# mLSTM gates turned by TensorE, and all retention state steps on GpSimd, in a two-block layer stack

## The chip, the cores and the metric

The program runs on one core of a Trainium2 chip. A core has TensorE (PE, matrix products and transposes into PSUM), VectorE (DVE), ScalarE (ACT), GpSimd (POOL) and SyncE (SP, which here issues the DMAs); each has its own list of instructions and runs it in order, and semaphores tie the lists together. The metric is the time of one execution in microseconds on the device (us).

## The reference, cut to what matters

Two blocks of two layers each work on 512 tokens of width 1024 in float32. The change touches the mLSTM's gates in the first block and the retention's states in the second.

```python
# first block, token_mixer: 4 mLSTM heads beside sliding-window attention
gates = mif + gate_bias                      # [512, 8]
log_i, log_f = gates[..., :4], log_sigmoid(gates[..., 4:])
ht = mlstm_chunkwise(mq_h, mk_h, mv_h, log_i, log_f)
# in it, for each chunk of 128 tokens:
bc = cumsum(log_f)                           # along the tokens
m_row = max(b + m, max(dlog))                # running maximum along the tokens
w_inter = exp(b + m - m_row); ws = exp(b_last - b + li - m_new)

# second block, bidirectional_retention: 6 heads, 4 chunks of 128 tokens, forward and backward
s_new = s * c_dec + einsum('bhcd,bhce->bhde', kb * k_dec, vb)
y = einsum(a, vb) + einsum('bhid,bhde->bhie', qb, s) * q_dec
```

## The kernel before

**Products.** Each float32 matrix product is made of three matmuls on split operands (L447 to L449: high by high, low by high, high by low). A weight tile comes by DMA on SP (L371), ACT rounds it to its high part (L385), DVE takes the low part (L386). PE's results lie in PSUM, in four buffers "mm" for products and four "ax" for transposes, scores and the like. Small work tiles named u come from a ring of 31 buffers (`NU`, L27): a new tile gets the buffer that has been free longest, and its first writer waits until the last user of that buffer is done.

**What sets the order.** The program is written out by a host loop. The products are emitted in units; each unit and each transpose moves a clock `s.now` forward by an estimate, and `s.later(delay, fn)` puts side work on a heap which is emitted once that clock has gone `delay` ns further. So a delay decides between which units, and behind which other instructions of its engine, a piece of side work stands. On the chip each engine then runs its list in that order, whatever the true times are.

**Gates, first block** (`gates1` to `gates4`, once a layer). `gates1` makes log_i and log_f as columns (tokens on partitions). To get rows (heads on partitions, tokens along the row), `gates2` writes them to device memory in eight DMAs whose elements are 4 bytes (L912), `gates3` reads them back as two tiles of 4x512 (L920). `gates4` then runs a scan over the tokens (the cumulative sum, L935), a subtraction (L936) and a small copy (L937); 1800 ns later `stab` has the second scan (the running maximum, L940) and four sums and differences (L941 to L944); `fin` writes five row tiles to device memory (L950), `cols` reads two of them back as columns in eight DMAs (L957), and `ends` takes their exponential (L962). `mlstm` fetches the other rows spread over partitions, and starts when the last product of its values is there.

**Beside it** in the same stretch run the units of the attention (scores by L581, the maximum by DVE's L1049, the exponential by ACT's L1054, the normalisation by L1059, L1060 and L593, transposes by L577, their copies by ACT's L1075 and DVE's L1077, the product with the values by L589) and `ev_qk`, which reads a product out of its "mm" buffer four times: ACT's L1243 and three convolution taps on DVE (L1246, 511, 510 and 509 columns).

**Retention, second block** (`x_layer`, once a layer). Tiles `st[0]` to `st[3]` hold the state at each chunk, the forward half on partitions 0 to 63 (`f`), the backward half on 64 to 127 (`b`). A step (`step`, L1357 and L1358) multiplies one half by its decay and adds it to the next tile: three steps forward on DVE, three backward on POOL, written out alternately. `ret_chunk` follows: two products of the queries with their decays (L1477), transposes of keys and queries whose copies are L1488, transposes of the decayed queries (L577, `dturn`), score products (L581), masks (L1511) and the output (L581).

**Modulation** (`mod`). When a layer's modulation is ready, `keep` writes four rows to device memory by four DMAs on SP in a row (L867).

Of the kernel before, what the change touches and what calls it, by code (L numbers as in the profile page):

```python
# [17 lines left out]
P = 128  # L18
# [188 lines left out]
class Net:  # L207
# [591 lines left out]
    def mod(s):  # L799
# [53 lines left out]
        def ready(l):  # L853
# [8 lines left out]
            def keep():  # L862
                gd = s.dram([2, 2, D], "mgate")
                for w in range(2):
                    for i in range(2):
                        o = (3 * i + 2) * 8
                        nc.sync.dma_start(gd[w, i].rearrange("(j p) -> p j", p=P), md[:, w, o:o + 8])  # L867
                s.mgate[l] = gd
# [22 lines left out]
    def gates1(s, l, zg, got):  # L891
# [13 lines left out]
        gd = s.dram([8, 512], "grow")  # L905
        s.later(6000, lambda: s.gates2(g3, lf3, gd, got))

    def gates2(s, g3, lf3, gd, got):
        nc = s.nc
        for i, src in enumerate((g3, lf3)):  # L910
            for t in range(NT):
                nc.sync.dma_start(gd[i * 4:i * 4 + 4, t * P:(t + 1) * P].rearrange("h p -> p h"), src[:, t, :4])  # L912
        s.later(3000, lambda: s.gates3(gd, got))

    def gates3(s, gd, got):
        nc = s.nc
        rows = []
        for i in range(2):
            r = s.u((4, 512))
            nc.sync.dma_start(r, gd[i * 4:i * 4 + 4])  # L920
            rows.append(r)
        s.later(2800, lambda: s.gates4(rows, got))

    def gates4(s, rows, got):
        nc = s.nc
# [13 lines left out]
        def stab():  # L939
# [5 lines left out]
            s.later(2600, fin)  # L945

        def fin():
            gr = s.dram([5, 4, 512], "gfin")
            for i, x in enumerate((bm, a, m, wi, ws)):
                nc.sync.dma_start(gr[i], x)  # L950
            s.later(2600, lambda: cols(gr))

        def cols(gr):
            co = s.ti(32)
            for i in range(2):
                for c in range(NT):
                    nc.sync.dma_start(co[:, i * 16 + c * 4:i * 16 + c * 4 + 4],  # L957
                                      gr[i, :, c * P:(c + 1) * P].rearrange("h p -> p h"))
            s.later(2800, lambda: ends(gr, co))

        def ends(gr, co):
            nc.scalar.activation(co[:, :16], co[:, :16], AF.Exp, scale=-1.0)  # L962
# [130 lines left out]
    def mlstm(s, gates, qk, vm, gs, outs):  # L1093
# [7 lines left out]
        def bring(hp):  # L1101
            for src, dst in ((4, wsb), (3, wib)):
# [5 lines left out]
        def bring_m(hp):  # L1108
            for i in range(2):
                w = s.u()  # L1110
                nc.sync.dma_start(w, gr[2, hp * 2 + i].partition_broadcast(P))
# [686 lines left out]
    def x_layer(s, l, xs, norm, res, mid, groups_of, sinks_of, parts):  # L1798
# [62 lines left out]
        yield from s.until(lambda: len(kv) == NT)  # L1861
# [259 lines left out]
```

## Time and profile before

| | |
|---|---|
| median of 3 runs | 2812.58 us (2811.86 to 2814.61) |
| profiled execution | 2813.32 us, span 2811.5 us |
| busy: PE | 2705.4 us, 96% of the span |
| busy: DVE | 1895.9 us, 67% |
| busy: ACT | 1167.0 us, 42% |
| busy: POOL | 572.0 us, 20% |
| mean granted clock of TensorE | 0.989 of full speed |

How to read it: the span is the time from the first to the last instruction of the profiled execution. PE is busy nearly all of it; its idle time is what waits cost. The list of waits says for an engine and line on whom they ended; the timeline has every instruction with its start, its length and the idle time before it, and the name behind the arrow is the instruction at which the awaited semaphore was last seen to rise, which can be the neighbour of the one that mattered.

### The profile page before, as it was taken

To read this page: it belongs to the slowest core of one execution; us is meant where nothing else is said; L and a number is where in the kernel's file an instruction comes from. 1 tells how busy PE (TensorE), PEld (TensorE's weight loads), DVE (VectorE), ACT (ScalarE), POOL (GpSimd) and SP (SyncE) were. 2 spreads that over 40 slices of the span, in tenths; PEclk is the share of its full clock that TensorE was granted. 3 is DMA by queue.
4 is the path that set the end of the run, shared out by engine and by line. 5 is a ranking of instruction groups with operands and counts; after the bars stand their busy time and mean duration, and the time that the engine had idled before them with its cause. 6 is when DMAs were issued, how large, how long until landed. Compare 5 with 4: busy or idle time off the path is not lost. (4 is left out here: it accounts for less than half of the span.)

```text
span 2811.5 us, 38854 instructions
## 1 busy us (share of the span) xinstructions
PE 2705.4 (96%) x14526; PEld 2291.8 (82%) x14526; DVE 1895.9 (67%) x3414; ACT 1167.0 (42%) x2098; POOL 572.0 (20%) x616
## 2 busy tenths in 40 slices
PE   8899999998999999999999999999999999999998
PEld 6678888876788887788788888888888888888887
DVE  6767777777668678857657787778646556664544
ACT  4555332445554323555443633223336442442433
POOL 2222000042230000234153220221102335201011
PEclk9999999999999999999999999999999999999999
DMA  5633444425334464333332243333513322333332
GB/s 166 89 90 124 148 153 140 145 77 86 91 112 153 149 124 158 123 118 113 105 92 82 87 139 117 105 117 109 87 49 98 116 73 73 97 118 100 98 98 68
DMA packets 135804, 308.22 MB, mean 110 GB/s; under 512 B 38024, under 2 KB 44040, under 8 KB 135616
## 3 DMA queue, kind: packets, MB, share of 16 engines
q1 hardware_dynamic: 135040, 304.69, 37.3%
q8 instruction: 115, 1.88, 0.3%
q10 hardware_dynamic: 576, 1.05, 0.1%
q14 instruction: 73, 0.60, 0.1%
HBM read 303.44 MB, written 2.24 MB: 109 GB/s over the span
## 5 line engine op out<-in xcount | busy, mean ns | idle before, releaser
L385 ACT CAST wh<-wr 128x1024 fp32r<-128x1024 f32 (+2 forms) x455 | 461.3, 1015 | 578.4 <-PE mm L449 259.6
L447 PE MATMUL mm<-nh,wh 128*128 128x512 f32 (+1 forms) x1776 | 671.6, 378 | 3.6 <-DVE nh L187 3.6
L448 PE MATMUL mm<-nl,wh 128*128 128x512 f32 (+1 forms) x1776 | 666.9, 375 | 0.9 <-POOL nl L188 0.4
L449 PE MATMUL mm<-nh,wl 128*128 128x512 f32 (+1 forms) x1776 | 665.9, 375 | 0.0
L386 DVE TENSOR_TENSOR wl<-wr,wh 128x1024 fp32r<-128x1024 f32 (+2 forms) x455 | 572.3, 1263 | 112.5 <-ACT wh L385 112.1
L617 DVE SCALAR_TENSOR_TENSOR u<-mm,vec,u 128x511 f32<-128x511 f32 (+2 forms) x440 | 305.9, 695 | 234.6 <-ACT u L612 163.5
L447 PE MATMUL mm<-wh,u 128*128 128x512 f32 (+1 forms) x1176 | 460.5, 392 | 2.1 <-ACT u L632 1.9
L448 PE MATMUL mm<-wl,u 128*128 128x512 f32 (+1 forms) x1176 | 454.7, 387 | 2.6 <-DVE wl L386 2.4
L449 PE MATMUL mm<-wh,u 128*128 128x512 f32 (+1 forms) x1176 | 454.4, 386 | 2.2 <-DVE u L633 1.5
L447 PEld LDWEIGHTS mm<-nh,wh 128*128 128x128 f32 x1776 | 336.6, 190 | 66.3 <-issue 4.8
L449 PEld LDWEIGHTS mm<-nh,wl 128*128 128x128 f32 x1776 | 336.0, 189 | 60.4
L448 PEld LDWEIGHTS mm<-nl,wh 128*128 128x128 f32 x1776 | 336.6, 190 | 58.1 <-DVE nl L188 1.0
L447 PEld LDWEIGHTS mm<-wh,u 128*128 128x128 f32 x1176 | 221.9, 189 | 46.8 <-ACT u L632 2.7
L449 PEld LDWEIGHTS mm<-wh,u 128*128 128x128 f32 x1176 | 221.6, 188 | 46.0 <-DVE u L633 3.5
L448 PEld LDWEIGHTS mm<-wl,u 128*128 128x128 f32 x1176 | 222.0, 189 | 45.3 <-DVE wl L386 5.0
L447 PE MATMUL mm<-wh,nh 128*128 128x384 f32 (+2 forms) x512 | 191.1, 373 | 17.2 <-DVE t L934 10.8
L577 PE MATMUL ax<-ident,u 128*128 128x128 f32 x930 | 137.4, 283 | 50.6 <-DVE u L154 18.3
L449 PE MATMUL mm<-wh,nl 128*128 128x384 f32 (+2 forms) x512 | 182.0, 355 | 1.5 <-POOL nl L188 1.5
L448 PE MATMUL mm<-wl,nh 128*128 128x384 f32 (+2 forms) x512 | 181.7, 355 | 0.0
L577 PEld LDWEIGHTS ax<-ident,u 128*128 128x128 f32 x930 | 108.5, 144 | 80.9 <-issue 25.0
L737 POOL TENSOR_TENSOR x<-x,u 128x512 f32<-128x512 f32 x64 | 103.2, 1613 | 342.6 <-DVE u L736 341.4
L572 POOL TENSOR_TENSOR t<-t,mhalf 128x1 f32<-128x1 f32 (+2 forms) x76 | 63.3, 835 | 508.1 <-DVE t L570 507.8
(248 smaller groups left out, 3703.9 us busy)
## 6 DMA issues: line engine op xcount, KB each, us to landing
wr<-in_up_dram SPq DMA_DIRECT2D x176, 512.0 KB
mrow<-in_wmod_dram SPq DMA_DIRECT2D x192, 256.0 KB
wr<-in_dn_dram SPq DMA_DIRECT2D x88, 512.0 KB
wr<-in_wo_dram SPq DMA_DIRECT2D x56, 512.0 KB
wr<-in_w2b_dram SPq DMA_DIRECT2D x56, 384.0 KB
wr<-in_w2a_dram SPq DMA_DIRECT2D x39, 512.0 KB
nab<-in_nab_dram SPq DMA_DIRECT2D x36, 128.0 KB
wr<-in_w1q_dram SPq DMA_DIRECT2D x8, 512.0 KB
```

Of the source, the lines that this page charges most:

```text
L385: nc.scalar.copy(h[:, :n], raw[:, :n])
L386: s.wlo[i] = lambda: nc.vector.tensor_sub(lo[:, :n], raw[:, :n], h[:, :n].bitcast(F32))
L447: mm(ps, ah, bh, start=first, stop=False)
L448: mm(ps, ah, bl, start=False, stop=False)
L449: mm(ps, al, bh, start=False, stop=last)
L572: nc.gpsimd.tensor_tensor(out=r, in0=e, in1=s.mhalf[:, :n], op=ALU.pow)
L577: s.nc.tensor.transpose(out, in_, s.ident[:p, :p])
L617: nc.vector.scalar_tensor_tensor(out=c[:, o], in0=ps[:, i], scalar=w[q], in1=c[:, o], op0=ALU.mult, op1=ALU.add)
L737: eng.tensor_add(x[:, c], x[:, c], o)
```

## The change

`gates1` now calls a single `gates2` after 7400 ns. It turns log_i and log_f by eight transposes on PE (4x128 each, into two "ax" buffers) and DVE copies the two 4x512 results (L920 in the changed file). `stab` stays 1800 ns behind; `fin` comes 4200 ns after it, writes three rows instead of five to device memory, and turns the other two into columns by eight transposes on PE (128x4); ACT takes the exponential from PSUM (L953) and DVE copies the rest (L954). The six retention steps all go to POOL, the three backward ones first. `keep`'s four DMAs come one every 4000 ns. Lines behind the gates move up by 8 (L1246 becomes L1238, L1357 and L1358 become L1349 and L1350, L1385 becomes L1377, L1477 becomes L1469, L1488 becomes L1480).

```diff
             def keep():
                 gd = s.dram([2, 2, D], "mgate")
-                for w in range(2):
-                    for i in range(2):
-                        o = (3 * i + 2) * 8
-                        nc.sync.dma_start(gd[w, i].rearrange("(j p) -> p j", p=P), md[:, w, o:o + 8])
-                s.mgate[l] = gd
+
+                def one(n):
+                    w, i = n // 2, n % 2
+                    o = (3 * i + 2) * 8
+                    nc.sync.dma_start(gd[w, i].rearrange("(j p) -> p j", p=P), md[:, w, o:o + 8])
+                    if n < 3:
+                        s.later(4000, lambda: one(n + 1))
+                    else:
+                        s.mgate[l] = gd
+                one(0)
...
-        gd = s.dram([8, 512], "grow")
-        s.later(6000, lambda: s.gates2(g3, lf3, gd, got))
-    def gates2(s, g3, lf3, gd, got):
...
-    def gates3(s, gd, got):
...
-    def gates4(s, rows, got):
+        s.later(7400, lambda: s.gates2(g3, lf3, got))
+
+    def gates2(s, g3, lf3, got):
         nc = s.nc
         rows = []
+        for src in (g3, lf3):
+            ps = s.ax()
+            for t in range(NT):
+                s.tr(ps[:4, t * P:(t + 1) * P], src[:, t, :4])
             r = s.u((4, 512))
-            nc.sync.dma_start(r, gd[i * 4:i * 4 + 4])
+            nc.vector.tensor_copy(r, ps[:4, :])
             rows.append(r)
...
-            s.later(2600, fin)
+            s.later(4200, fin)
...
-            gr = s.dram([5, 4, 512], "gfin")
-            for i, x in enumerate((bm, a, m, wi, ws)):
+            gr = s.dram([3, 4, 512], "gfin")
+            for i, x in enumerate((m, wi, ws)):
                 nc.sync.dma_start(gr[i], x)
-            s.later(2600, lambda: cols(gr))
...
+            ps = s.ax()
+            for i, x in enumerate((bm, a)):
                 for c in range(NT):
...
+                    o = i * 16 + c * 4
+                    s.tr(ps[:, o:o + 4], x[:, c * P:(c + 1) * P])
+            co = s.ti(32)
+            nc.scalar.activation(co[:, :16], ps[:, :16], AF.Exp, scale=-1.0)
+            nc.vector.tensor_copy(co[:, 16:], ps[:, 16:32])
...
-        for c in range(NT - 1):
-            s.step(nc.vector, rc, f, st[c + 1], st[c])
-            d = NT - 1 - c
+        for d in range(NT - 1, 0, -1):
             s.step(nc.gpsimd, rc, b, st[d - 1], st[d])
+        for c in range(NT - 1):
+            s.step(nc.gpsimd, rc, f, st[c + 1], st[c])
```

**DVE at the gates of layer 0, before**, from the copy of the attention's transposes to the first scan (u_986 is the tile that the convolution builds, mm_872 the "mm" buffer it is read from, t_943 to t_956 belong to the normalisations):

```order
L1077 COPY u_975<-ax_970 128x512
L1246 SCALAR_TENSOR_TENSOR u_986<-mm_872,vec_72,u_986 128x511
L1059 TENSOR_TENSOR t_943<-t_943,t_944 128x2
L1060 RECIPROCAL t_945<-t_943 128x2
L593 TENSOR_SCALAR u_941<-u_941,t_945 128x256
L1246 SCALAR_TENSOR_TENSOR u_986<-mm_872,vec_72,u_986 128x510
L1059 TENSOR_TENSOR t_954<-t_954,t_955 128x2
L1060 RECIPROCAL t_956<-t_954 128x2
L593 TENSOR_SCALAR u_952<-u_952,t_956 128x256
L1246 SCALAR_TENSOR_TENSOR u_986<-mm_872,vec_72,u_986 128x509
L934 MEMSET t_1013 4x1
L935 SCALAR_TENSOR_TENSOR u_1010<-u_1012,u_981 4x512
```

After, the same stretch begins so (ax_968 and ax_975 hold the turned gates, u_982 and u_984 are tiles of the scans; L931 is the first scan):

```order
L1069 COPY u_966<-ax_961 128x512
L920 COPY u_973<-ax_968 4x512
L920 COPY u_980<-ax_975 4x512
L930 MEMSET t_985 4x1
L931 SCALAR_TENSOR_TENSOR u_982<-u_984,u_980 4x512
L932 TENSOR_TENSOR u_973<-u_973,u_982 4x512
L933 COPY u_983<-u_982 4x3
```

The first scan and what belongs to it stood behind the third tap and now stand ahead of the first. A little further on DVE's list now has (mm_871 is the "mm" buffer of the taps; L936 is the second scan):

```order
L593 TENSOR_SCALAR u_932<-u_932,t_936 128x256
L1238 SCALAR_TENSOR_TENSOR u_998<-mm_871,vec_72,u_998 128x511
L1238 SCALAR_TENSOR_TENSOR u_998<-mm_871,vec_72,u_998 128x510
L1051 TENSOR_TENSOR t_945<-t_945,t_946 128x2
L1052 RECIPROCAL t_947<-t_945 128x2
L593 TENSOR_SCALAR u_943<-u_943,t_947 128x256
L936 SCALAR_TENSOR_TENSOR u_984<-u_983,u_973 4x512
L937 TENSOR_TENSOR t_985<-u_982,u_984 4x4
L938 TENSOR_TENSOR u_983<-u_982,u_984 4x512
L939 TENSOR_TENSOR u_980<-t_985,u_984 4x512
L940 TENSOR_TENSOR u_982<-u_973,u_984 4x512
L1238 SCALAR_TENSOR_TENSOR u_998<-mm_871,vec_72,u_998 128x509
```

The second scan and the four operations behind it (L937 to L940) stood behind the next attention unit and now stand between the second and the third tap.

**DVE at the retention of layer 0 in the second block, before**, with the engines or queues on which each instruction waits in brackets (u_13096 to u_13099 are `st`, u_13547 the queries of chunk 0, t_13081 the decays):

```order
L1357 TENSOR_TENSOR u_13599<-u_13096,t_13081 64x384 [waits DVE_49,Pool_49]
L1358 TENSOR_TENSOR u_13097<-u_13097,u_13599 64x384 [waits DVE_49]
L1357 TENSOR_TENSOR u_13605<-u_13097,t_13081 64x384 [waits DVE_49,Pool_49]
L1358 TENSOR_TENSOR u_13098<-u_13098,u_13605 64x384 [waits DVE_49]
L1357 TENSOR_TENSOR u_13611<-u_13098,t_13081 64x384 [waits DVE_49,Pool_49]
L1358 TENSOR_TENSOR u_13099<-u_13099,u_13611 64x384 [waits DVE_49]
L1385 TENSOR_TENSOR u_13576<-u_13576,u_13577 128x384
L1385 TENSOR_TENSOR u_13594<-u_13594,u_13595 128x384
L386 TENSOR_TENSOR wl_13590<-wr_13521,wh_13589 128x1024 [waits DMAHW0_49,PE_49]
L1477 TENSOR_TENSOR u_13671<-u_13547,t_13080 128x384 [waits DVE_49]
```

After, without the steps (u_13549 are the queries of chunk 0):

```order
L1377 TENSOR_TENSOR u_13578<-u_13578,u_13579 128x384 [waits Pool_49]
L1377 TENSOR_TENSOR u_13596<-u_13596,u_13597 128x384 [waits DVE_49,Pool_49]
L386 TENSOR_TENSOR wl_13592<-wr_13523,wh_13591 128x1024 [waits DMAHW0_49,PE_49]
L1469 TENSOR_TENSOR u_13673<-u_13549,t_13082 128x384 [waits DMAHW3_49,DVE_49,Pool_49]
L1469 TENSOR_TENSOR u_13675<-u_13549,t_13082 128x384 [waits Pool_49]
L1480 COPY u_13681<-ax_13677 128x384 [waits PE_49,Pool_49]
L1480 COPY u_13687<-ax_13683 128x384 [waits PE_49]
```

POOL's list after, at the same place (u_13098 to u_13101 are `st`; u_13601 to u_13616 are the six products):

```order
L1349 TENSOR_TENSOR u_13601<-u_13101,t_13083 64x384 [waits DVE_49,Pool_49]
L1350 TENSOR_TENSOR u_13100<-u_13100,u_13601 64x384 [waits Pool_49]
L1349 TENSOR_TENSOR u_13604<-u_13100,t_13083 64x384 [waits DVE_49,Pool_49]
L1350 TENSOR_TENSOR u_13099<-u_13099,u_13604 64x384 [waits Pool_49]
L1349 TENSOR_TENSOR u_13607<-u_13099,t_13083 64x384 [waits Pool_49]
L1350 TENSOR_TENSOR u_13098<-u_13098,u_13607 64x384 [waits Pool_49]
L1349 TENSOR_TENSOR u_13610<-u_13098,t_13083 64x384 [waits DVE_49]
L1350 TENSOR_TENSOR u_13099<-u_13099,u_13610 64x384 [waits Pool_49]
L1349 TENSOR_TENSOR u_13613<-u_13099,t_13083 64x384 [waits Pool_49]
L1350 TENSOR_TENSOR u_13100<-u_13100,u_13613 64x384 [waits Pool_49]
L1349 TENSOR_TENSOR u_13616<-u_13100,t_13083 64x384 [waits Pool_49]
L1350 TENSOR_TENSOR u_13101<-u_13101,u_13616 64x384 [waits Pool_49]
```

The six instructions of DVE's steps have gone to the end of POOL's; the first L1469 and the one behind it, and the first L1480, now wait for POOL, where before the first L1477 waited for DVE alone and the second for PE. In the ring of 31, u_13673 has the buffer that u_13610 had, u_13675 that of u_13613, and u_13681 that of u_13616.

## Rows read from the trace of the kernel before

**Rows 1.** PE's waits: waiting tile and line <- releaser: us in total, times, longest

```profile
PE mm L447 <- DVE t L934: 10.8, 2, 5.4
PE ax L577 <- DVE u L1477: 10.3, 2, 5.2
...
PE ax L589 <- ACT u L1075: 7.3, 6, 3.0
...
PE ax L577 <- DVE u L1124: 2.7, 2, 1.4
```

**Rows 2.** PE timeline, layer 0 gates: start, us, instruction, [idle before <-releaser]

```profile
93.18 1.09 PE L577 MATMUL ax<-ident,u 128*128 128x128 f32 x8
94.03 0.47 PE L447 MATMUL mm<-wh,nh 128*128 128x512 f32 x1
...
101.73 0.77 PE L447 MATMUL mm<-wh,nh 128*128 128x512 f32 x1 [5.38 <-DVE t L934]
...
110.10 1.53 PE L589 MATMUL ax<-u,u 128*64 128x128 f32 x24 [1.12 <-ACT u L1075]
```

**Rows 3.** Timeline of DVE in the same stretch

```profile
95.30 0.68 DVE L1077 COPY u<-ax 128x512 f32<-128x512 f32 x1
98.20 0.75 DVE L1246 SCALAR_TENSOR_TENSOR u<-mm,vec,u 128x511 f32<-128x511 f32 x1 [2.22 <-ACT u L1243]
...
100.84 0.74 DVE L1246 SCALAR_TENSOR_TENSOR u<-mm,vec,u 128x509 f32<-128x509 f32 x1
...
103.69 1.21 DVE L935 TENSOR_TENSOR_SCAN u<-u,u 4x512 f32<-4x512 f32 x1 [2.11 <-DMA u<-grow]
...
105.62 1.20 DVE L386 TENSOR_TENSOR wl<-wr,wh 128x1024 fp32r<-128x1024 f32 x1
...
109.68 1.91 DVE L940 TENSOR_TENSOR_SCAN u<-u,u 4x512 f32<-4x512 f32 x1
...
113.51 0.14 DVE L1059 TENSOR_TENSOR t<-t,t 128x2 f32<-128x2 f32 x1
```

**Rows 4.** Timeline of PE at the same place of layer 1

```profile
689.77 0.77 PE L447 MATMUL mm<-wh,nh 128*128 128x512 f32 x1 [5.44 <-DVE t L934]
...
696.81 1.53 PE L589 MATMUL ax<-u,u 128*64 128x128 f32 x24 [0.23 <-ACT u L1075]
```

**Rows 5.** Timeline of DVE at the retention steps, second block, layer 0

```profile
1487.51 0.95 DVE L1381 TENSOR_TENSOR u<-u,cos 128x384 f32<-128x384 f32 x1
1488.56 0.55 DVE L1357 TENSOR_TENSOR u<-u,t 64x384 f32<-64x384 f32 x1
...
1496.08 1.65 DVE L1385 TENSOR_TENSOR u<-u,u 128x384 f32<-128x384 f32 x2
1497.66 1.21 DVE L386 TENSOR_TENSOR wl<-wr,wh 128x1024 fp32r<-128x1024 f32 x1
1498.79 1.81 DVE L1477 TENSOR_TENSOR u<-u,t 128x384 f32<-128x384 f32 x2
1500.53 1.01 DVE L1488 COPY u<-ax 128x384 f32<-128x384 f32 x2
```

**Rows 6.** Timeline of POOL in the same stretch

```profile
1489.84 0.83 POOL L1357 TENSOR_TENSOR u<-u,t 64x384 f32<-64x384 f32 x1 [1.80 <-DVE u L1358]
1490.75 1.00 POOL L1358 TENSOR_TENSOR u<-u,u 64x384 f32<-64x384 f32 x1
...
1496.29 1.02 POOL L1357 TENSOR_TENSOR u<-u,t 64x384 f32<-64x384 f32 x1 [1.31 <-DVE u L1358]
1497.40 2.32 POOL L1358 TENSOR_TENSOR u<-u,u 64x384 f32<-64x384 f32 x1
```

**Rows 7.** Timeline of PE in the same stretch

```profile
1500.19 1.54 PE L577 MATMUL ax<-ident,u 128*128 128x128 f32 x6 [5.13 <-DVE u L1477]
1501.66 1.65 PE L581 MATMUL ax<-u,u 64*128 64x128 f32 x12
```

**Rows 8.** Window after that stall: length, busy by engine, PEclk, DMA share, GB/s

```profile
1502.00:1504.00 2.00, 2.00 (x14) 1.78 (x13) 1.32 (x3) 0.32 (x1) 0.00 (x0) 0.50 0.37 35
```

More of the change, by code (lines that the diff above doesn't have):

```diff
@@ L904, in gates1 @@
         nc.vector.scalar_tensor_tensor(out=lf3, in0=g3[:, :, 4:], scalar=0.0, in1=t3, op0=ALU.min, op1=ALU.subtract)
-        gd = s.dram([8, 512], "grow")
-        s.later(6000, lambda: s.gates2(g3, lf3, gd, got))
-    def gates2(s, g3, lf3, gd, got):
[L909 to L913, printed above, removed]
-    def gates3(s, gd, got):
+        s.later(7400, lambda: s.gates2(g3, lf3, got))
+    def gates2(s, g3, lf3, got):
         nc = s.nc
         rows = []
-        for i in range(2):
+        for src in (g3, lf3):
+            ps = s.ax()
+            for t in range(NT):
+                s.tr(ps[:4, t * P:(t + 1) * P], src[:, t, :4])
             r = s.u((4, 512))
-            nc.sync.dma_start(r, gd[i * 4:i * 4 + 4])
+            nc.vector.tensor_copy(r, ps[:4, :])
             rows.append(r)
-        s.later(2800, lambda: s.gates4(rows, got))
-    def gates4(s, rows, got):
-        nc = s.nc
         li, lfr = rows
@@ L944, in stab @@
             nc.vector.tensor_sub(ws3, a3, m3[:, :, P - 1:].to_broadcast([4, NT, P]))
-            s.later(2600, fin)
+            s.later(4200, fin)
         def fin():
-            gr = s.dram([5, 4, 512], "gfin")
-            for i, x in enumerate((bm, a, m, wi, ws)):
+            gr = s.dram([3, 4, 512], "gfin")
+            for i, x in enumerate((m, wi, ws)):
                 nc.sync.dma_start(gr[i], x)
-            s.later(2600, lambda: cols(gr))
-        def cols(gr):
-            co = s.ti(32)
[L955 to L962, printed above, removed]
+            ps = s.ax()
+            for i, x in enumerate((bm, a)):
+                for c in range(NT):
+                    o = i * 16 + c * 4
+                    s.tr(ps[:, o:o + 4], x[:, c * P:(c + 1) * P])
+            co = s.ti(32)
+            nc.scalar.activation(co[:, :16], ps[:, :16], AF.Exp, scale=-1.0)
+            nc.vector.tensor_copy(co[:, 16:], ps[:, 16:32])
             got["gates"] = (co[:, :16], gr, co[:, 16:])
@@ L1101, in bring @@
         def bring(hp):
-            for src, dst in ((4, wsb), (3, wib)):
+            for src, dst in ((2, wsb), (1, wib)):
                 w = s.u()
@@ L1110, in bring_m @@
                 w = s.u()
[L1111 removed]
+                nc.sync.dma_start(w, gr[0, hp * 2 + i].partition_broadcast(P))
                 dec[hp * 2 + i] = w
@@ L1861, in x_layer @@
         yield from s.until(lambda: len(kv) == NT)
+        for d in range(NT - 1, 0, -1):
+            s.step(nc.gpsimd, rc, b, st[d - 1], st[d])
         for c in range(NT - 1):
-            s.step(nc.vector, rc, f, st[c + 1], st[c])
-            d = NT - 1 - c
-            s.step(nc.gpsimd, rc, b, st[d - 1], st[d])
+            s.step(nc.gpsimd, rc, f, st[c + 1], st[c])
         def ev_gate(t, ps):
```

## The prediction

> **What bounds the kernel now.** I read the page's busy times and the list of PE's waits first, then the timelines of the stretches in which the longest of these waits lie. PE is at work for 96% of the span, so only what lengthens or shortens PE's own list, or a wait in it, moves the end. Of the waits, the change touches four kinds [rows 1]: the matmul L447 on DVE's L934 (10.8 us, twice), L577 on L1477 (10.3 us, twice), L589 on ACT's L1075, and L577 on L1124 (2.7 us, twice, in the mLSTM). SP, whose issues the change thins out most, feeds none of the long ones.
>
> The name of a releaser is to be read with care. L934 is a memset that nothing of PE's needs. The matmul at 101.73 takes the fourth "mm" buffer, and the last reader of that buffer is the third convolution tap, L1246 on 509 columns, just ahead of L934 on DVE: 100.84 + 0.74 = 101.58, and PE goes on 0.15 us later [rows 2, 3]. That tap is late because tap 1 waits for ACT (2.22 us idle, L1243), and each tap has a normalisation ahead of or behind it. The gates' trip through memory ends later still (the scan L935 idles 2.11 us for it), with PE already running. **So the DMAs that go were not what held PE.**
>
> **Gates, first block (two layers).** Gone are 20 DMA issues a layer and the scan's wait. Added on PE are 16 transposes a layer; a batch of eight steps 0.85 us here (93.18 to 94.03) [rows 2]. The first eight (4x128) fall before the stall and cost PE nothing, since PE then waits for tap 3 anyhow; if that cover went, they would cost 0.85. The other eight (128x4) come after it on PE's path: 0 to 0.85, and I take 0.8, as the row is for the same instruction.
>
> What DVE does is the larger term. In the changed order two copies, the memset, scan, subtraction and small copy stand ahead of tap 1, and the second scan with its four followers stands between tap 2 and tap 3. PE waits for tap 3 as before, so all of this comes before it. By rows 3: L1077 ends at 95.98; two copies of 512 elements a row at L1077's 0.68 each to 97.3; scan, subtraction and small copy 1.93 (103.69 to 105.62) to 99.2; ACT's L1243 was done by 98.2, so it no longer sets the time; normalisation, taps 1 and 2, normalisation 2.64 (98.20 to 100.84) to 101.9; second scan and followers 3.83 (109.68 to 113.51) to 105.7; tap 3 0.74 to 106.5, PE at 106.6. Before it went on at 101.73: **+4.9 us**. Layer 1 has the same stall (5.44) behind the same rows [rows 4], so +4.9 there too. Given back: the wait of L589 for L1075, 1.12 in layer 0 and 0.23 in layer 1 [rows 2, 4], as the scan's wait no longer delays the softmax behind it. Per layer: 4.9 + 0.8 - 1.1 = 4.6 and 4.9 + 0.8 - 0.2 = 5.5, **together +10.1**. Bounds: copies of four rows at half price and the small transposes free, +7; PE's half speed after the longer stall lasting as long again as now, +13. What is queued behind tap 3 on DVE (L386, the L1049 of the next unit) moves with PE, and no other engine waits for it meanwhile.
>
> **mLSTM.** The key transposes now come behind ten matmul units instead of six, so L577's wait for L1124 (2.7 us in both layers, [rows 1]) should go, while the turns behind the last chunk follow each other more closely and may wait instead. I take half of it, -1.3, between -4 and +1.4 (one such wait more).
>
> **mgate.** Four small DMAs 4 us apart instead of in a row. They are spread between weight fetches on SP's queue, and none of PE's waits in [rows 1] ends on a weight; PE's cover is the weights already fetched ahead. I take 0, and -1 to +1 as an estimate of what a late fetch could move.
>
> **Retention steps, second block (two layers).** Before, DVE and POOL take turns, since both halves lie in the same tiles; DVE then does L1385 twice, L386, L1477 twice, and PE, idle for 5.13 us, starts its transposes on L1477 at 1500.19 and its products on the L1488 copies at 1501.66 [rows 5, 7]. With the steps off DVE one would expect L1477 long before PE is ready, and the wait gone. The changed order says otherwise. The small tiles turn in a ring of 31 buffers, where a new tile takes the one that came free longest ago. The six products of the steps, now all on POOL, are the last to come free, and the first L1469 (L1477 before) now waits for a POOL semaphore as well as DVE's own: its output takes the buffer of the fourth step's product. The second takes the fifth's, the first L1480 copy the sixth's. So **DVE waits for POOL's fourth, fifth and sixth step**, with the copies, an L386 and L1503 queued behind.
>
> When do these end? POOL can begin when DVE's L1381 is through, 1487.51 + 0.95 = 1488.5 [rows 5]. The first step has the company that the third POOL step had before, L1385 twice and L386: 1496.29 to 1499.72, 3.43 us [rows 6]; it ends at 1492.0. A step alone takes 0.91 + 1.00 + 0.09 = 2.0 (1489.84 to 1491.75 and the gap) [rows 6]: the fourth ends at 1498.0. The first L1469 runs beside the fifth step (L1357 at 1.02 instead of 0.83), so that ends at 1500.2, the sixth at 1502.4. Two copies at 1.01 [rows 5] end at 1503.4, and PE's products start at 1503.5 instead of 1501.66: **+1.9 a layer, +3.8**. PE's six transposes fall into the wait. Its clock is at half (0.50) from 1500 on [rows 8] and would be in the same state, for the same work. Bounds: the first step not hindered, 1.5 less; hindered by every DVE instruction for its whole length, 0.83 + 1.00 + 1.65 + 1.21 = 4.7 for the first step, 1.3 more; half speed 1 us longer or 1.5 shorter: -1 to +4.2 a layer.
>
> How much POOL is hindered can be read both from a row and from a rule. The row: L1358 took 2.32 beside L386 (1.21) and 1.00 alone, while L1357 took only 1.02 beside the two L1385 [rows 5, 6]. The Trainium skill, "SBUF — State Buffer", section "Who interferes with whom", says that a DVE instruction with two inputs in SBUF and a GpSimd one that reads it lock each other out for a whole instruction. L386 agrees with that, the L1385 don't; by the rule the sum would be 1.3 more a layer, an estimate. The measured step decides. Another page of the Trainium skill speaks against moving the steps at all: "GPSIMD Engine Reference", section "Engine selection", puts elementwise products and sums on VectorE, with GPSIMD about 2 times slower for two inputs; here L1357 takes 0.83 on POOL against 0.55 on DVE, 1.5 times [rows 5, 6]; at 2 times the four steps up to the first L1469 would end later still.
>
> **Sum.** 10.1 - 1.3 + 0 + 3.8 = +12.6 us. The profiled execution took 2813.3 (span 2811.5), which would become 2825.9; the median of the three runs is 0.7 lower, so **2825 us**.
>
> **Rivals.**
> *The retention wait goes* (the not-slower side). If L1469 found its buffer free, DVE would be through at 1488.5 + 1.65 + 1.21 + 1.81 + 1.01 = 1494.2 [rows 5], before PE runs dry at 1500.19 - 5.13 = 1495.06 [rows 7]. Then 5.1 a layer goes, and with it the half speed behind it: six L577 take 1.54 where eight take 1.09 at full speed [rows 2, 7], so 0.7 on these, as much on the twelve products (1.65) and 1 on the matmuls behind them by the same ratio, 2.4 in all: -15, and with the gates 2813.3 + 8.8 - 15 = 2807, or 2806 against the median. It decides if POOL's fourth step ends before 1494. For it speaks that DVE has nothing else to do until then; against it stand the wait for POOL in the order and 3.43 + 3 x 2.0 = 9.4 us of POOL's work before that step's end. 6%.
> *The gates' stall goes.* If PE hung on L934 as the list says, and the gates came early enough, -10.8 takes the place of the two 4.9: 2825.9 - 9.8 - 10.8 = 2805. Against it stands the buffer that the matmul takes. 4%. Both together: about 2786, 2%.
> *Lower costs all at once*: POOL unhindered (0.4 a layer), gates at +7, mLSTM at -3: 2813.3 + 5 = 2818, no difference to be measured. 11%.
> *POOL locked out for every instruction of DVE's, or the half speed lasting longer at all four stalls*: 2825.9 + 2.6 to + 6, 2828 to 2832. 9%.
> My forecast, both stalls longer: 68%.
>
> **How the numbers follow.** About 0.2% (5.6 us) is what a measurement of this kernel tells from no change. Faster by more than that are the first two rivals: 12%. Within it: the low-cost case and a little of the forecast's lower edge, 13%. Slower: 75%. The forecast's own range is 2817 to 2831; with a part of the low case and the locked-out case 2815 to 2832 leaves out no more than 2 in 10.
>
> **What would show it.** Right: PE's two stalls in front of the fourth "mm" buffer of 9 to 10 us each, with tap 3 behind L936 to L940 on DVE; PE's wait at L577 on L1469 still there, with DVE idle some 6 us on POOL's L1350 before it; L581 a good 8 us after PE ran dry. Wrong: L1469 running at about 1491 (then the ring doesn't bind), POOL steps of much less or more than 2.0, tap 3 ahead of the second scan, or new PE waits in the mLSTM of over 2 us.

## The result, and the profile after

| | before | after |
|---|---|---|
| median | 2812.66 us (4 runs, 2811.86 to 2814.61) | 2830.87 us (4 runs, 2827.80 to 2836.46) |
| profiled execution | 2813.32 us | 2833.06 us |
| mean granted clock of TensorE | 0.989 | 0.982 |

The ratio is 1.0066, with a 95% interval of 1.0048 to 1.0084: the change makes the kernel slower, by 18 us, where 12.6 were forecast. The time lies in the predicted range, near its upper end.

PE's waits in the profile of after, as [rows 1] for before (waiting tile and line, releaser, us in total, times, longest):

```profile
PE mm L447 <- DVE u L1238: 16.1, 2, 8.1
PE ax L577 <- DVE u L1469: 10.0, 4, 3.3
PE ax L589 <- ACT u L1067: 5.9, 4, 3.0
PE ax L581 <- DVE u L1480: 3.8, 2, 1.9
PE mm L447 <- ACT u L632: 3.4, 2, 2.5
```

The first answers to L447 on L934 (10.8), the second to L577 on L1477 (10.3); L581 on L1480 is new; the wait of L577 for L1124 (2.7) is gone from the list. L589 on ACT has lost 1.4, but it stands at 5.9 in the profiles of experiments 4, 9 and 12 too, whose gates are those of before, so that loss is not shown to be the change's.

**Gates.** PE's timeline after, at the fourth "mm" buffer of layers 0 and 1 (start, us, instruction, idle before it):

```profile
105.89 0.77 PE L447 MATMUL mm<-wh,nh 128*128 128x512 f32 x1 [8.06 <-DVE u L1238]
...
696.35 0.77 PE L447 MATMUL mm<-wh,nh 128*128 128x512 f32 x1 [8.03 <-DVE u L1238]
```

and DVE's timeline after, in layer 0, which answers to [rows 3]:

```profile
95.84 1.27 DVE L920 COPY u<-ax 4x512 f32<-4x512 f32 x2
...
97.21 1.21 DVE L931 TENSOR_TENSOR_SCAN u<-u,u 4x512 f32<-4x512 f32 x1
...
99.78 1.53 DVE L1238 SCALAR_TENSOR_TENSOR u<-mm,vec,u 128x511 f32<-128x511 f32 x2
...
101.87 1.20 DVE L936 TENSOR_TENSOR_SCAN u<-u,u 4x512 f32<-4x512 f32 x1
...
105.02 0.73 DVE L1238 SCALAR_TENSOR_TENSOR u<-mm,vec,u 128x509 f32<-128x509 f32 x1
```

Nothing on DVE waits any more between 95.2 and 105.7; the third tap simply has the copies and both scans ahead of it, and PE goes on 0.14 us behind it (105.02 + 0.73 = 105.75). The second scan with its followers takes 3.15 us (101.87 to 105.02), not the 3.83 of the sum: the scan itself takes 1.20, where L940 of before took 1.91 [rows 3]. The stall is 2.7 us longer in layer 0 and 2.6 in layer 1.

**Retention.** DVE's timeline after, layer 0 of the second block, answers to [rows 5]:

```profile
1498.99 0.96 DVE L1373 TENSOR_TENSOR u<-u,cos 128x384 f32<-128x384 f32 x1
1499.87 1.65 DVE L1377 TENSOR_TENSOR u<-u,u 128x384 f32<-128x384 f32 x2
1501.44 2.03 DVE L386 TENSOR_TENSOR wl<-wr,wh 128x1024 fp32r<-128x1024 f32 x1
1509.23 0.56 DVE L1469 TENSOR_TENSOR u<-u,t 128x384 f32<-128x384 f32 x1 [5.75 <-POOL u L1350]
1511.57 0.56 DVE L1469 TENSOR_TENSOR u<-u,t 128x384 f32<-128x384 f32 x1 [1.78 <-POOL u L1350]
1513.90 1.02 DVE L1480 COPY u<-ax 128x384 f32<-128x384 f32 x2 [1.78 <-POOL u L1350]
```

POOL's timeline in the same stretch, the first, the second, the fourth and the fifth step (product, then sum) and the sum of the sixth:

```profile
1500.09 1.01 POOL L1349 TENSOR_TENSOR u<-u,t 64x384 f32<-64x384 f32 x1 [0.56 <-DVE u L1373]
1501.18 1.21 POOL L1350 TENSOR_TENSOR u<-u,u 64x384 f32<-64x384 f32 x1
1502.47 1.69 POOL L1349 TENSOR_TENSOR u<-u,t 64x384 f32<-64x384 f32 x1
1504.25 1.01 POOL L1350 TENSOR_TENSOR u<-u,u 64x384 f32<-64x384 f32 x1
...
1507.31 0.82 POOL L1349 TENSOR_TENSOR u<-u,t 64x384 f32<-64x384 f32 x1
1508.21 0.98 POOL L1350 TENSOR_TENSOR u<-u,u 64x384 f32<-64x384 f32 x1
1509.27 1.20 POOL L1349 TENSOR_TENSOR u<-u,t 64x384 f32<-64x384 f32 x1
1510.55 0.98 POOL L1350 TENSOR_TENSOR u<-u,u 64x384 f32<-64x384 f32 x1
...
1512.88 0.99 POOL L1350 TENSOR_TENSOR u<-u,u 64x384 f32<-64x384 f32 x1
```

and PE's, which answers to [rows 7]:

```profile
1509.84 0.74 PE L577 MATMUL ax<-ident,u 128*128 128x128 f32 x3 [3.31 <-DVE u L1469]
1512.18 0.90 PE L577 MATMUL ax<-ident,u 128*128 128x128 f32 x3 [1.60 <-DVE u L1469]
1514.98 1.65 PE L581 MATMUL ax<-u,u 64*128 64x128 f32 x12 [1.90 <-DVE u L1480]
```

The fourth step ends at 1509.19 and the first L1469 starts at 1509.23; the fifth at 1511.53, the second L1469 at 1511.57; the sixth at 1513.87, L1480 at 1513.90. DVE waits for three of POOL's steps in turn, and what links them is the ring: its output tiles take the buffers of their products (experiment 4 is the test).

**The clock.** Four windows of 2 us in the profile of after (length, busy time of PE, PEld, DVE, ACT and POOL, then the granted clock, DMA share, GB/s), two of layer 0 and two of layer 1:

```profile
1510.00:1512.00 2.00, 0.58 (x3) 0.18 (x2) 0.43 (x1) 0.00 (x0) 1.84 (x3) 0.52 0.00 0
1520.00:1522.00 2.00, 2.00 (x19) 2.00 (x18) 0.00 (x0) 0.00 (x0) 0.00 (x0) 0.92 0.74 254
2372.00:2374.00 2.00, 0.55 (x3) 0.31 (x3) 0.47 (x1) 0.00 (x0) 1.92 (x2) 0.91 0.00 0
2390.00:2392.00 2.00, 2.00 (x11) 2.00 (x10) 0.61 (x2) 0.49 (x1) 0.00 (x0) 0.82 0.00 0
```

Between the two of each pair the clock is at 0.50 (1.2 of 2.4 GHz), before and behind them at 1.00. A window's mean tells when it changed: 0.52 is half speed for 0.96 of the window, so the clock fell at 1510.1; by the same working it rose at 1520.3, fell at 2373.6 and rose at 2390.7. That is 10.2 us at half speed in layer 0 and 17.1 in layer 1, where before it was 6.8 in both (worked out from the windows of the same kind around [rows 8]). PE is busy without a gap in the last twelve of those 17 us. By the same working the half clock at the two stalls of the gates lasted 10.2 us each after, and 6.8 each before.

The same matmuls take nearly twice as long at half clock, as the 24 products L581 behind the retention's stall of layer 1 show, first in the profile of after and then in that of experiment 11, where the clock was back by then:

```profile
2381.34 5.21 PE L581 MATMUL ax<-u,u 128*128 128x64 f32 x24
```

```profile
2372.88 2.79 PE L581 MATMUL ax<-u,u 128*128 128x64 f32 x24
```

So a stall costs more than the idle time that the list of waits shows. Between the two profiles (spans of 2811.5 and 2831.3 us) PE's idle time, the span less its busy time on the page, grew by 5.8 us, from 106.1 to 111.9. Its busy time at half clock, added up over the whole trace, grew by 24.0, from 47.7 to 71.7; at 2.79 to 5.21 that is a loss of about 11 us, an estimate. The 2.9 that remain are about what 32 transposes more take (eight take 0.85 [rows 2]).

### The profile page after: what moved, and what is told of

Same layout as the page of the kernel before. It is cut to its first block, busy times and chain, and to the rows that moved or that the text cites. A ratio compares the mean times of both kernels' runs of the same rounds, so it can differ in the third digit from the quotient of the medians.

```text
span 2831.3 us, 38861 instructions
## 1 busy us (share of the span) xinstructions
PE 2719.4 (96%) x14558; PEld 2303.0 (81%) x14558; DVE 1891.1 (67%) x3408; ACT 1168.1 (41%) x2098; POOL 587.1 (21%) x628
## 3 DMA queue, kind: packets, MB, share of 16 engines
q10 hardware_dynamic: 576, 1.05, 0.1%
## 5 line engine op out<-in xcount | busy, mean ns | idle before, releaser
L447 PE MATMUL mm<-nh,wh 128*128 128x512 f32 (+1 forms) x1776 | 672.6, 379 | 3.6 <-DVE nh L187 3.6
L386 DVE TENSOR_TENSOR wl<-wr,wh 128x1024 fp32r<-128x1024 f32 (+2 forms) x455 | 573.4, 1266 | 108.8 <-ACT wh L385 108.3
L447 PE MATMUL mm<-wh,u 128*128 128x512 f32 (+1 forms) x1176 | 462.0, 393 | 4.4 <-ACT u L632 3.4
L447 PEld LDWEIGHTS mm<-nh,wh 128*128 128x128 f32 x1776 | 337.2, 190 | 66.4 <-issue 4.8
L447 PEld LDWEIGHTS mm<-wh,u 128*128 128x128 f32 x1176 | 223.0, 190 | 49.4 <-ACT u L632 4.2
L447 PE MATMUL mm<-wh,nh 128*128 128x384 f32 (+2 forms) x512 | 192.5, 376 | 22.1 <-DVE u L1238 16.1
L577 PE MATMUL ax<-ident,u 128*128 128x128 f32 (+1 forms) x946 | 138.1, 282 | 45.5 <-DVE u L154 17.0
L577 PEld LDWEIGHTS ax<-ident,u 128*128 128x128 f32 (+1 forms) x946 | 109.4, 144 | 75.7 <-issue 18.6
```

What stands on the lines that cost most here:

```text
L386: s.wlo[i] = lambda: nc.vector.tensor_sub(lo[:, :n], raw[:, :n], h[:, :n].bitcast(F32))
L447: mm(ps, ah, bh, start=first, stop=False)
L577: s.nc.tensor.transpose(out, in_, s.ident[:p, :p])
```

## The experiments

Experiments 1 to 4, 5 to 8, 9 and 10, and 11 and 12 are four groups, each on one chip with its own runs of the kernel before; a saving or cost in us is the ratio's distance from 1 times 2813. A kernel built on the one before keeps its line numbers or shifts them by a few: L1238 of after is L1233 where `keep` is as before, L1469 is L1464 or L1477.

**1. The retention edit alone.** The two loops of steps as changed, all else as before.

```diff
-        for c in range(NT - 1):
-            s.step(nc.vector, rc, f, st[c + 1], st[c])
-            d = NT - 1 - c
+        for d in range(NT - 1, 0, -1):
             s.step(nc.gpsimd, rc, b, st[d - 1], st[d])
+        for c in range(NT - 1):
+            s.step(nc.gpsimd, rc, f, st[c + 1], st[c])
```

> The retention edit alone on the kernel before: all six state steps on POOL, gates and modulation as before. Theory (the ring of 31 makes DVE wait for POOL's fourth, fifth and sixth step): PE's products L581 start 15.0 us after DVE's last L1381 instead of 13.2, so +1.9 us a layer, and PE stays at half clock somewhat longer: +4 to +8 us in all, 2817 to 2821. DVE idles about 5.7 us at L1477 on POOL's L1358. Rival (the steps off DVE free PE, and the changed kernel lost its time elsewhere): PE's 5.1 us waits go, -10 to -15, about 2800.

Measured: 2823.18 us (2821.33 to 2825.26) where before was 2813.32; ratio 1.0041 (1.0029 to 1.0053), so 8 to 15 us. The waits are those of after (L577 on L1477 9.8 us in four pieces, L581 on L1488 3.8 in two). The mechanism is there and the price is two to four times the forecast's 3.8. Little of it is idle time: in the profile PE idles 107.9 us, 1.8 more than before, but the half clock behind the two stalls lasts 10.2 and 17.1 us, as in after, where before had 6.8 twice. The granted clock of its five runs is 0.983 to 0.985, that of the 23 runs of before on the same chip 0.986 to 0.991.

**2. The gates edit alone.** As in the change, with the steps and `keep` of before.

> The gates edit alone on the kernel before: turned by TensorE, retention and modulation as before. Theory (scans between the taps): PE's stall ahead of the fourth mm buffer grows from 5.4 to about 8.1 us in each layer, 16 transposes more; partly given back in the mLSTM by L1124's waits: +4 to +6 us, 2817 to 2819. The prediction's own terms give +8.8, 2821. Rival (the gates' DMAs were what PE waited for): the stall shrinks and the time falls below 2810.

Measured: 2816.23 (2813.37 to 2820.47), ratio 1.0015 (1.0006 to 1.0025), 2 to 7 us. The stalls are those of after, 8.07 and 8.03 us:

```profile
PE mm L447 <- DVE u L1233: 16.1, 2, 8.1
```

**3. The modulation edit alone.** `keep`'s four writes spread as in the change, all else as before.

> The modulation edit alone on the kernel before: four small DMAs 4 us apart instead of in a row. The prediction gave it 0 (-1 to +1), 2812.6. Theory after the trace of the changed kernel: each of the four now stands between weight fetches on SP's queue, ACT's casts of the up weights wait 5 to 7 us for their DMA instead of 1.4, and PE waits 1.5 us more at L447 on L632: +1.5 to +5 us with the clock that falls there, 2814 to 2818.

Measured: 2815.87 (2810.16 to 2823.64), ratio 1.0015 (1.0004 to 1.0026), 1 to 7 us. One wait of PE is longer in its profile, L447 on ACT's L632 (1.9 in both layers together before):

```profile
PE mm L447 <- ACT u L632: 2.9, 2, 2.1
```

**4. The retention edit with the products out of the ring.** `step` takes a tile for its product, and the six calls of `x_layer` give it `fin`, which is there already and free by then.

```diff
-    def step(s, eng, rc, hs, dst, src):
+    def step(s, eng, rc, hs, dst, src, t=None):
...
-        t = s.u((P, 384))
+        t = s.u((P, 384)) if t is None else t
...
-            s.step(nc.gpsimd, rc, b, st[d - 1], st[d])
+            s.step(nc.gpsimd, rc, b, st[d - 1], st[d], fin)
```

> As e1_ret_only, but the six products of the steps are written to the tile fin, which is not used any more by then, instead of six tiles of the ring. Theory of the ring: L1477 no longer waits for POOL and runs at once behind L386, PE's 5.1 us wait and the half clock behind it go in both layers: -10 to -16 us, 2797 to 2803. Rival (POOL's steps are late by themselves, for the state st[0] that the output needs, or by sharing with DVE): the wait moves to L581 on POOL's L1358 and the time stays within 3 us of e1_ret_only.

Measured: 2802.57 (2799.68 to 2805.95), ratio 0.9966 (0.9954 to 0.9978): 10 us faster than before, 21 faster than experiment 1. The long waits at L577 and L581 are gone; what is left:

```profile
PE ax L577 <- DVE u L1488: 2.3, 2, 1.1
...
PE ax L581 <- DVE u L1488: 0.6, 2, 0.3
```

POOL is no faster here than in the change (its six steps take 15.8 us in layer 0, and 13.8 there); only DVE no longer waits for it. That settles the ring as the cause of the retention's stall.

**5. The gates edit with the second scan put off.** As experiment 2, with two delays changed; on DVE's list the third tap then stands ahead of the second scan.

```diff
-            s.later(4200, fin)
+            s.later(2400, fin)
...
-        s.later(1800, stab)
+        s.later(3600, stab)
```

> The gates edit alone, as in the kernel before otherwise, but the second scan is put off by 3600 ns instead of 1800 and the last part by 2400 instead of 4200. On DVE's list the third tap then stands ahead of the second scan and its four followers, and nothing else of the first scan moves. Theory (PE's stall is the sum of what DVE does ahead of the third tap): the two stalls before the fourth mm buffer fall by the 3.15 us that the second scan and its followers took, from 8.05 to about 4.9 each, and the time by 6 us against the gates edit alone, to 2810 (2807 to 2813) where the kernel before is at 2813. Rival (the stall is set by the turned gates or by ACT): stalls stay near 8, 2816. Second rival (the scan, put off, is missed later on): stalls at 4.9, but a new wait of PE of 2 to 3 us a layer at L589 or in the mLSTM, 2813 to 2816.

Measured: 2812.25 (2808.99 to 2814.47), ratio 0.9994 (0.9985 to 1.0002), 5.9 us less than experiment 2 by the two ratios. DVE's timeline and PE's waits of this kernel:

```profile
101.40 0.74 DVE L1233 SCALAR_TENSOR_TENSOR u<-mm,vec,u 128x509 f32<-128x509 f32 x1
...
103.19 1.20 DVE L931 TENSOR_TENSOR_SCAN u<-u,u 4x512 f32<-4x512 f32 x1
```

```profile
PE mm L447 <- DVE u L1233: 9.8, 2, 4.9
```

Each stall is 3.1 us shorter, the 3.15 of the second scan and its followers: the stall is the sum of what stands ahead of the third tap.

**6. Experiments 4 and 5 together**, `keep` as before.

> The previous kernel's gates and the retention steps on POOL with their products in a tile of their own (fin), the four modulation writes in a row as before. Theory (the parts add up): the ratio of the steps with fin (0.9966) times that of the late gates (about 0.999) gives 0.9955, 2800 us (2796 to 2804). Rival (the gains share one cover, TensorE's half clock after stalls): no better than the steps with fin alone, 2803 to 2806.

Measured: 2799.01 (2797.40 to 2800.81), ratio 0.9948 (0.9936 to 0.9961). The parts add up (0.9966 x 0.9994 = 0.9960), and this version is 15 us faster than before and 33 faster than the change.

**7. The change with `keep`'s writes in a row again.**

> The changed kernel with the four modulation writes in a row again, all else as changed. Theory (spreading them costs what it cost alone, 1 to 7 us): 2826.5 (2824 to 2829). Rival (what it cost alone was the phase of the clock's dips, not the writes): as the changed kernel, 2830 to 2832.

Measured: 2830.03 (2826.77 to 2832.28), ratio 1.0055 (1.0041 to 1.0068), against 1.0066 (1.0048 to 1.0084) of the change: the intervals overlap, and neither theory is excluded. L447 waits 1.0 at L632 again.

**8. The change with the products in `fin`**, the edit of experiment 4 on the whole change.

> The changed kernel, all three edits, with the products of the retention steps written to the tile fin instead of six buffers of the ring. Theory (the ring makes the retention's stall within the whole change too): the two waits at L577 and the long one at L581 go, and the time falls by the 20.6 us that it fell with the retention edit alone, 2810 (2806 to 2814): faster than the kernel before in spite of the gates' longer stalls. Rival (with the gates' delay in front, POOL is later than PE anyway): a wait of 2 to 4 us a layer stays, 2816 to 2824.

Measured: 2806.82 (2803.55 to 2807.95), ratio 0.9977 (0.9968 to 0.9987): 25 us less than the change, and faster than before. The gates' stalls are unchanged, the retention's are gone:

```profile
PE mm L447 <- DVE u L1238: 16.1, 2, 8.1
...
PE ax L577 <- DVE u L1480: 2.3, 2, 1.1
```

**9. Before, with the products in `fin` alone.** DVE and POOL take the steps as before.

```diff
-            s.step(nc.vector, rc, f, st[c + 1], st[c])
+            s.step(nc.vector, rc, f, st[c + 1], st[c], fin)
             d = NT - 1 - c
-            s.step(nc.gpsimd, rc, b, st[d - 1], st[d])
+            s.step(nc.gpsimd, rc, b, st[d - 1], st[d], fin)
```

> The kernel before with one edit: the products of the six steps, still taken in turns by DVE and POOL, go to the two halves of the tile fin instead of six ring tiles. Theory (the turns that DVE and POOL took before came from the ring too): each engine runs its three steps without waiting for the other, DVE is through with them about 3.5 us after L1381 instead of 7.6, PE's stall at L577 falls from 5.1 us to 1 to 3, and the time to 2803 (2800 to 2808). Rival (the turns come from the state tiles that both halves share, as the prediction had it): DVE still idles 2.1 us twice on POOL, the stall stays at 5 us, 2812 to 2814. Second rival (both engines at once hinder each other by as much as the turns cost): no idle time between steps, but steps of 1.5 to 2 us on DVE, 2809 to 2813.

Measured: 2812.47 (2810.35 to 2817.18), ratio 0.9999 (0.9990 to 1.0008). DVE's and POOL's timelines, pieces of the steps and what follows on DVE, and PE's behind them:

```profile
1489.07 1.18 DVE L1357 TENSOR_TENSOR fin<-u,t 64x384 f32<-64x384 f32 x1
1490.28 1.26 DVE L1358 TENSOR_TENSOR u<-u,fin 64x384 f32<-64x384 f32 x1
1491.57 1.07 DVE L1357 TENSOR_TENSOR fin<-u,t 64x384 f32<-64x384 f32 x1
...
1496.25 1.01 DVE L1385 TENSOR_TENSOR u<-u,u 128x384 f32<-128x384 f32 x2
...
1498.32 1.01 DVE L1477 TENSOR_TENSOR u<-u,t 128x384 f32<-128x384 f32 x2
```

```profile
1489.91 1.21 POOL L1358 TENSOR_TENSOR u<-u,fin 64x384 f32<-64x384 f32 x1
```

```profile
1498.92 1.54 PE L577 MATMUL ax<-ident,u 128*128 128x128 f32 x6 [3.29 <-DVE u L1477]
```

The idle times of 2.09 us in which DVE waited for POOL's L1358 are gone, so the turns, too, came from the ring. But each of DVE's instructions now takes 1.07 to 1.26 us, where it took 0.55 with POOL idle [rows 5], and its three steps together 7.2 us (1489.07 to 1496.25) where they took 7.5 with the turns (1488.56 to 1496.08). The stall is shorter (3.29 for 5.13) because POOL is done by then and L1385 and L1477 run at 1.01 for 1.65 and 1.81; the time doesn't show it. In this profile PE idles 99.0 us, 7.1 less than before, but is busy at half clock for 58.8 us where before has 47.7, which takes back about 5. This is the second rival, with steps of about 2.4 us on DVE and not of 1.5 to 2.

**10. Experiment 9 with the late gates.** It differs from experiment 6 only in who does the steps, and in their order.

> The kernel before with the late gates edit and the steps in turns on DVE and POOL with products in fin: it differs from the steps on POOL with fin and late gates only by who does the forward steps and by the order of the steps. Theory (with the ring out of the way POOL has time for all six, DVE has little): 2 to 8 us above that kernel, 2801 to 2807. Rival (once the ring is out of the way it is all the same who does the steps): 2799, within 2.

Measured: 2812.06 (2807.89 to 2814.93), ratio 0.9991 (0.9983 to 1.0000), 12 us above experiment 6, and so above both expectations: who does the steps matters more than expected, once the ring is out of the way. L577 waits 6.4 us on DVE's L1464, a wait that experiment 6 hasn't. PE's idle time in the two profiles is 96.1 us here and 90.2 there, its busy time at half clock 58.8 and 40.5.

**11. The change once more, for a second profile.**

> The changed kernel once more, for a second profile. In the first, TensorE's granted clock was at half (0.50) after the retention's stall from 1510.1 to 1520.3 in layer 0 and from 2373.6 to 2390.7 in layer 1. Theory (how long the clock stays down belongs to this kernel's schedule at that place): about 10 us in layer 0 and 17 us in layer 1 again, within 1 us. Rival (it depends on the run, by where the stall happens to fall): other lengths, by 3 us or more, in at least one layer, with the same stalls.

Measured: 2820.19 us, one run, where before took 2807.84 on the same chip. The waits of PE at the gates and at the retention are the same to 0.1 us as in the first profile (16.1; 9.9; 3.8); L447 on L632 waits 1.9 and not 3.4. The half clock lasted 10.2 us in layer 0 again, and in layer 1 only from 2365.8 to 2372.7:

```profile
2364.00:2366.00 2.00, 0.55 (x3) 0.31 (x3) 0.22 (x2) 0.00 (x0) 1.84 (x3) 0.96 0.00 0
...
2372.00:2374.00 2.00, 2.00 (x15) 2.00 (x15) 1.20 (x2) 0.00 (x0) 0.00 (x0) 0.83 0.53 215
```

6.8 us, not 17.1: the rival. PE's idle time is 109.2 us where the first profile has 111.9, its busy time at half clock 46.9 where that has 71.7; the two together are worth about 14 us by the rate above, and the spans differ by 12.9.

**12. Experiment 9 once more, for a second profile.**

> The steps in turns on DVE and POOL with products in fin once more, for a second profile. In the first, the stall at L577 was 3.29 and 3.19 us in the two layers, and the half clock behind it lasted from 1498.7 to 1502.1 in layer 0 and from 2355.4 to 2369.1 in layer 1. Theory (belongs to the schedule): 3.4 us and 13.7 us again, within 1 us. Rival (depends on the run): other lengths in at least one layer with the same stalls, which would make the time of a single run of this kernel differ by some us.

Measured: 2807.65 us, one run (before 2807.84). The stalls are the same (3.17 and 3.19). Behind the one in layer 1 the half clock lasted 3.4 us, 2356.4 to 2359.8, not 13.7:

```profile
2356.00:2358.00 2.00, 1.82 (x14) 1.27 (x13) 2.00 (x4) 0.96 (x2) 0.00 (x0) 0.59 0.82 219
2358.00:2360.00 2.00, 2.00 (x13) 1.78 (x12) 1.39 (x4) 0.00 (x0) 0.00 (x0) 0.56 0.54 109
```

Again the rival. The chips of experiments 9 and 12 differ, but within experiment 9's one profile the two layers, with stalls of 3.29 and 3.19 us, already had 3.4 and 13.7 us.

## Why the prediction was right, and where it was not

The sign and both mechanisms were right. That the total is near is in part luck, because errors of both signs met. The forecast's terms against the runs of each part alone:

| term | forecast | measured alone |
|---|---|---|
| gates and mLSTM | +10.1 - 1.3 = +8.8 | +4.2 (1.7 to 7.0) |
| mgate | 0 (-1 to +1) | +4.2 (1.1 to 7.3) |
| retention | +3.8 (-2 to +8.4) | +11.5 (8.2 to 14.9) |
| sum | +12.6 | +19.9; the whole change +18.6 (13.5 to 23.6) |

- *The stall at the fourth "mm" buffer.* Right in mechanism: the releaser in before's list, a memset, was not the reason, and the third tap was. Experiment 5 shows it, since moving only the second scan behind the tap takes 3.1 us from each stall. In size the forecast was 106.6 for PE's return and the trace has 105.89. The mis-sized term is the second scan, priced at 1.91 by the one row of it, while the first scan of the same shape stood at 1.21 beside it in [rows 3]. Here they take 1.21 and 1.20. The prediction's sign of stalls of 9 to 10 us wasn't met either: they are 8.1, since the second scan is shorter and PE runs dry later, at 97.8 for 96.4, by two groups of turns of 0.60 us and a wait of 0.41.
- *What comes back.* The net cost of the first block was taken as 4.6 and 5.5 us a layer at L589, less 0.65 for the mLSTM. In the two profiles the same matmul starts at 20.60 and 20.04 ahead of layer 0's gates and at 245.73 and 246.95 behind its mLSTM: +1.8. For layer 1 the pairs are 608.00 and 609.20, then 820.62 and 825.50: +3.7. So 5.5 and not 8.8. L577's waits for L1124 went, as said; that the turns behind them would wait more instead, for which half of the gain was held back, didn't happen. The shorter second scan in both layers is most of the rest. The 1.1 and 0.2 us that were to come back at L589 are a matter of the run: with the gates of before the wait at that matmul of layer 0 is 1.12 and 1.13 us in the profiles of before and of experiment 3, and missing in those of experiments 1, 4, 9 and 12.
- *mgate at nothing.* The cover was named as the weights already fetched. ACT's casts show that it isn't whole. ACT's timeline of after, then that of before, at the first layer's up weights:

```profile
1062.04 1.05 ACT L385 CAST wh<-wr 128x1024 fp32r<-128x1024 f32 x1 [5.39 <-DMA wr<-in_up_dram]
1070.22 1.05 ACT L385 CAST wh<-wr 128x1024 fp32r<-128x1024 f32 x1 [7.13 <-DMA wr<-in_up_dram]
```

```profile
1060.15 1.05 ACT L385 CAST wh<-wr 128x1024 fp32r<-128x1024 f32 x1 [1.50 <-DMA wr<-in_up_dram]
```

  The last line of each is the fourth cast of its group. Before, the first cast of the group waits long (15.14 us) and the next three follow closely. After, counted from the cast of an earlier group (1032.10 before, 1037.87 after), the group starts 5.4 us sooner and its fourth cast comes 4.3 us later. PE's L447 then waits 2.5 for 1.05 us on ACT's L632 some 40 us on. In the four profiles with the edit (after, experiments 3, 8 and 11) that cast is 4.3, 3.9, 3.9 and 2.8 us late and that wait 2.5, 2.1, 2.1 and 1.0 us; in the ten without it the wait is 1.0 each time. In layer 1 the four writes still stand in a row (one entry of four in SP's queue at 2006.03), since SP has no other issue between them. The direct loss is 1.0 to 1.5 us once, and none in experiment 11; whether the rest of the 4.2 is real stays open, as experiment 7 doesn't separate it from nothing and the profiled run of experiment 3 took 2811.74 us, less than the 2813.32 of before.
- *The ring.* Right, and the steps of the working with it. From the end of DVE's L1373 (1499.95) POOL's fourth step ends 9.2 us later and the sixth 13.9, where the forecast had 9.5 and 13.9 behind L1381; L581 starts 15.0 us behind L1373's end where it was 13.2 behind L1381's before, +1.8 for a forecast of +1.9. Two errors inside cancelled: the first step took 2.30 and not 3.43, the second 2.8 and not 2.0. L386 took 2.03 for 1.21 with the sum of the first step in front, and POOL's next product 1.69 for 0.83 with L386 beside it: each delayed the other.
- *A reason that was wrong.* The prediction said that DVE and POOL took turns because both halves lie in the same tiles. Experiment 9 leaves the state tiles alone and the turns go. It was the ring in the kernel before, too. The reading that the two L1385 don't agree with the lock-out looked at POOL's side alone: they took 1.65 us beside POOL and 1.01 without it (experiment 9).
- *The step that failed in size* is the one on the clock in the retention's term: "would be in the same state, for the same work", with bounds of 1 us longer and 1.5 shorter. The direct waits cost what was forecast. In the first profile of after, layer 1 lost 1.8 us up to L581 and 4.1 more behind it, on the same work at half speed until 2390.7. In the second profile, where the clock was back after 6.8 us, the retention cost +1.6 us in layer 0 and +1.4 in layer 1 against before (offsets of the same matmuls ahead of the stall and behind it), 3.0 for a forecast of 3.8. The longer half clock is the more usual outcome: in layer 1 it lasted 17.1 us in three of the four profiles with this stall (after, experiments 1 and 7) and 6.8 in one (experiment 11), in layer 0 10.2 in all four, and the runs of experiment 1 cost 8 to 15 us in all.
- *The rivals.* "The retention wait goes" was priced at 7.5 us a layer (5.1 of stall and 2.4 of half clock). Its condition, that the ring doesn't bind, was made true in experiment 6, and there the layer's gain is 7.6 us (the same matmul is 1.9 us earlier than in before at 1281.88 and 9.5 earlier at 1508.30). In that layer of that profile the price was right; the whole kernel gained 10 us from it (experiment 4), not 15. In the change the condition didn't hold. The rival that did come about is one given 9%, "the half speed lasting longer at all four stalls", for 2828 to 2832: in the first profile of after it lasted 10.2, 10.2, 10.2 and 17.1 us at the four stalls, where before had 6.8 at each, and the median of 2830.87 lies in that range. In experiment 11 it was longer at three of the four.
- *Who should do the steps.* The Trainium skill, "GPSIMD Engine Reference", section "Engine selection", was cited against the move, for its 2 to 1 in favour of DVE. Experiments 6 and 10 speak for the move here: with the ring out of the way six steps on POOL are 12 us cheaper than three on each, as DVE is on PE's path there and POOL isn't. No run has all six on DVE, which is what the Trainium skill would have; an instruction of them takes DVE 0.55 us alone [rows 5], so the twelve would take about 7 with the gaps between them, an estimate, as long as DVE's six took beside POOL in experiment 9. The other page of the Trainium skill cited, "SBUF — State Buffer", section "Who interferes with whom", has a DVE instruction with two inputs and a GpSimd one shut each other out. Experiment 9 agrees that they delay each other (DVE 1.07 to 1.26 us for 0.55 alone, POOL 1.02 to 1.21 for 0.83 and 1.00), but not for the whole of their durations: three steps of each took 7.2 us side by side, and 8.8 would be the sum of their times alone. The 1.3 us a layer that the rule would have added didn't come either.

## What to carry to other kernels

When work moves to a slower engine, look at who gets its scratch buffers next: a ring that hands out the buffer free longest ties the engine that was to be relieved to the one that took the work, and a scratch tile of its own undid it here, 25 us on the whole change. Find what really ends a wait from the buffer that the waiting instruction takes, not from the releaser's name, and count everything that an edit puts ahead of that instruction on the releasing engine. A delay that moved one scan behind the instruction PE waits for was worth 6 us; what the saved memory round trips are worth beside it is not clear of noise (0.9994, 0.9985 to 1.0002). And look at the clock beside the waits: by the estimate above, more than half of what this change cost in its first profile is time that PE lost by working at half clock.

## What the runs showed of the hardware

Behind the same stall, of the same kernel, TensorE's half clock lasted 17.1 us in one run and 6.8 in another (experiment 11), and 13.7 and 3.4 (experiment 12), and within one run 10.2 and 17.1, or 3.4 and 13.7, in two layers with the same code. The two profiled executions of after differ by 12.9 us with the same waits at the gates and at the retention, those of before that belong to them by 5.5. The Trainium skill, "TensorE: Matmul & The Clock Gate", section "Part 1: The HAM clock gate", says of a kernel's start that the number of matmuls at the lower clock changes from run to run; the traces show the like behind stalls. What sets the length in a run stays open. So a stall of a few us has no fixed price here, and a term of this kind needs a median over several runs and not one profile.

DVE and POOL instructions of 64x384 elements that overlap took 1.0 to 1.3 us each, where DVE's takes 0.55 and POOL's 0.83 and 1.00 alone. Three steps of each side by side took 7.2 us in experiment 9, and 7.5 in turns before, so that running both engines at once gained little. And a copy of four rows of 512 elements from PSUM took 0.67 us on average (1.27 for two in a row), nearly the 0.69 of 128 rows.
